# A decoder layer with an mLSTM: another place in memory and another queue for its first head's loads

## Chip, cores and metric

The kernel runs on one core of one Trainium2 chip. The metric is the device time of one execution in microseconds (us), as a median of several. Lower is better.

## What is computed

One hybrid decoder layer over 1024 tokens of width 1024, all in f32. It has three parts, each added to the residual `x`, with a shift, a scale and a gate that are made from a vector `c` for each part:

```
x = x + 0.5*(1+gate0) * swiglu_1(norm(x))
u = norm(x) @ w_in                              # inputs of both kinds of heads
x = x + (1+gate1) * concat(attention(u), mlstm(u)) @ w_out
x = x + 0.5*(1+gate2) * swiglu_2(norm(x))
```

The middle part has 4 heads of differential attention and 4 heads of an mLSTM, each 128 wide. The mLSTM's queries and keys come from `u` through a causal convolution over 4 tokens and a silu; its values come from `u` directly. The mLSTM is computed in chunks:

```
W   = (q k^T) * exp(D - m)                      # in a chunk, masked
num = e_inter * (q C) + W v                     # C: state of 128x128 carried on
h   = num / max(|den|, exp(-m))
C   = decay * C + k^T (w * v)
out = sigmoid(o) * rmsnorm(h) * g
```

where `o`, the output gate, is another product of `u`.

## The kernel before

The kernel is written on a framework that takes instructions in program order, gives tiles their addresses, sets the semaphores, and plans the order of the instructions of each engine: it plays the program on its own clock, and an engine takes the earliest instruction, in program order, of those that are ready by that clock. `high_priority` moves instructions up. An engine then runs its list strictly in order. DMAs are listed on the queue of the engine that issues them: SP (`nc.sync`), ScalarE (`nc.scalar`) or GpSimd (`nc.gpsimd`).

Matrix products are made of three passes each, with a high and a low part of both operands (`mm3`, lines 192 to 194), and two by two blocks are multiplied by Winograd's scheme (`wino`). In the order of the program, the middle of the kernel does this:

- products for values, queries and keys of attention, which are stored to DRAM (`davd`, `qkd`);
- the products of the mLSTM's values, transposed in tiles `vt` and stored to DRAM (`mlv`);
- the products of the mLSTM's queries and keys with the convolution (`conv_handlers`): inputs in tiles `cu`, results in tiles `cv`, stored to DRAM (`mlqk`);
- the products of the output gate (`o_handlers`): each of 8 half heads goes through a tile `vc` (lines 222, 770, 771) and is stored to DRAM (`mlo`, line 772);
- then the pools of all this are closed and new ones opened. `attn_load(0)` loads attention's first head in fourteen DMAs on GpSimd's queue (lines 785 to 789: `oq`, two kinds of `ok`, and `dav`, by halves of 512 tokens), and the heads follow.

`ml_head(h)` is one mLSTM head. It loads keys, queries and values (`mk`, `mq`, `mv`, lines 876 to 878; 512 KB each), head 0 on ScalarE's queue and the others on SP's. `weights` makes decay masks (L889, L891) and their exponentials `mE` (L894), the products of keys and queries (L898), `mW` (L900), and the transposed and weighted keys `kw` (L905, L908). `state` multiplies `kw` with the values (L914), and `read` gathers the outputs in `mn`. In the tail of a head `so` loads the output gate back (L971). `attn_head` does blocks of 128 queries: scores `s` (L807 to L809), maximum, exponentials, transposes and the product with values. The heads of both kinds are independent, so the planner mixes them.

Memory is a stack with two sides. A pool has a range of bytes in every partition, and its tags get rising addresses inside it in the order in which they are first requested; a tag has `bufs` buffers in a row. Pools that come later lie on the bytes of closed ones. With `reuse_waits="tile"`, a tile waits for the users of the earlier tiles on its own bytes. The ranges that matter here, in bytes of a partition, in the kernel before:

| Pool | Tag and range |
|---|---|
| tmp (closed at the boundary) | k: up to 173952 |
| mle (closed at the boundary) | six `vc` of 2048 bytes: 173952 to 186240; two `vt`: 186240 to 190336 |
| nothing at that time | 190336 to 198112 |
| cvp (closed at the boundary) | four `cu`: 198112 to 214604; two `cv`: 214624 to 222816 |
| mlp (opened at the boundary) | mE 170464, mW 174560, mn 178656, mq 186976, mk 195168, mv 203360, mssq 211680, kw 211744, mC 215840, other small ones, so 218720 to 222816 |

In mlp each tag has two buffers (mC four), 4096 bytes each for mq and mk, 4160 for mn and mv, 2048 for mE, mW, kw and so. Head 0 has the first buffer of each and head 1 the second. The gate half that is made last (head 3) is written to the `vc` at 182144; an earlier half of the same head to the one at 173952.

The mE and mW tiles that are requested right after mlp is opened are never written. They only make mE and mW the first tags of the pool.

Of the kernel before, what the change touches and what calls it, by code (L numbers as in the profile page):

```python
# [16 lines left out]
F32 = mybir.dt.float32  # L17
# [8 lines left out]
P = 128  # L26
# [100 lines left out]
class Layer:  # L127
# [739 lines left out]
        return self.y_put(0, h, hf, y)  # L867


    def ml_head(self, h):  # L870
        nc = self.nc
        tl = lambda n, s, **k: self.mlp.tile(s, F32, tag=n, name=n, **k)
        N = tl("mn", [P, 8, 130])
        q, k, v = tl("mq", [P, T]), tl("mk", [P, T]), tl("mv", [P, 8, 130])
        queue = nc.sync if h else nc.scalar
        queue.dma_start(out=k, in_=self.mlqk[4 + h])
        queue.dma_start(out=q, in_=self.mlqk[h])
        queue.dma_start(out=v[:, :, 0:P], in_=self.mlv[h])
        nc.vector.memset(v[:, :, P:130], 1.0)
        sc = P ** -0.5  # L880
        ssq = tl("mssq", [P, 8])
        Ws, kws, Cs = [], [], [None]
# [43 lines left out]
        def read(cs):  # L926
            three = lambda t: t[:, 0:130 * len(cs)].rearrange("p (a b) -> p a b", b=130)
            n = N[:, cs[0]:cs[-1] + 1, :]
            has = [c for c in cs if c > 0]
            I = self.ps()  # L930
            for i, c in enumerate(cs):
                if c > 0:
                    nc.tensor.matmul(I[:, 130 * i:130 * i + 130], cut(q, c), Cs[c], start=True, stop=True,
                                     skip_group_check=True)
            o = cs[0] == 0
            nc.vector.tensor_tensor(out=N[:, has[0]:has[-1] + 1, :], in0=three(I)[:, has[0] - cs[0]:, :],
                                    in1=self.cols[:, 2, has[0]:has[-1] + 1, h:h + 1].broadcast_to([P, len(has), 130]),
# [5 lines left out]
            if o:  # L943
                nc.scalar.copy(out=N[:, 0, :], in_=J[:, 0:130])
            nc.vector.tensor_tensor(out=N[:, has[0]:has[-1] + 1, :], in0=N[:, has[0]:has[-1] + 1, :],
                                    in1=three(J)[:, has[0] - cs[0]:, :], op=ALU.add)
            for c in cs:
                junk = tl("junk2", [P, P], bufs=1)
                nc.scalar.activation(out=junk, in_=N[:, c, 0:P], func=AF.Square, accum_out=ssq[:, c:c + 1])

# [9 lines left out]
        def tail():  # L960
            d, dr, dt = tl("md", [P, 8]), tl("mr", [P, 8]), tl("mt", [P, 8])
            den = N[:, :, P:P + 1].rearrange("p c o -> p (c o)")
            nc.vector.scalar_tensor_tensor(out=d, in0=den, scalar=-1.0, in1=den, op0=ALU.mult, op1=ALU.max)
# [26 lines left out]
def build(tc, yT, **A):  # L990
    nc = tc.nc
    with ExitStack() as es:
        L = Layer(tc, A, es)
# [272 lines left out]
        L.ep = apool("ep", bufs=5)  # L1266
        L.atp = apool("atp", bufs=2)
        L.mlp = rpool("mlp", bufs=2)
        for n in ("mE", "mW"):
            L.mlp.tile([P, 4, P], F32, tag=n, name=n)  # L1270
        L.aops = L.attn_load(0)
        L.ml_tail = lambda: None
        for kind, h in [("m", h) for h in range(4)] + [("a", h) for h in range(4)]:
# [105 lines left out]
```

## Time and profile before

| What | us |
|---|---|
| median of 3 runs (2024.95 to 2032.16) | 2028.65 |
| the profiled execution | 2029.4 |
| its span in the trace | 2027.6 |

The mean granted clock of TensorE was 0.978 of full speed in the profiled execution. Times in the views are microseconds from the start of the span, `x` is a count of instructions, and L898 is line 898 of the kernel. PE is TensorE, PEld its weight loads, DVE VectorE, ACT ScalarE, POOL GpSimd and SP the sync engine; a `q` behind a name means its queue of DMA issues. PEclk is the clock that TensorE was granted, as a part of full speed. The landing of a DMA is recorded for GpSimd's queue alone; for the others it shows in what waits for it.

### The profile page before, as it was taken

The numbers are of one execution on the slowest core, as the hardware profiler recorded it, in microseconds if no ns is written. First come the engines' busy times: TensorE is split into PE (matmuls) and PEld (weight loads), VectorE is DVE, ScalarE is ACT, GpSimd is POOL, SyncE is SP. The second block draws the span as 40 slices with busy tenths as digits, with TensorE's granted clock in tenths as the row PEclk, the third lists the DMA queues.
The fourth block names the chain that finished last, engine by engine and source line by source line (L and its number), as shares of the span: only waits on it lengthen the run. The fifth ranks groups of instructions, "written<-read, shape, count | busy, mean of one in ns | idle before, by whom it ended". The sixth has DMA issues, their size and how long they took to land.

```text
span 2027.6 us, 24626 instructions
## 1 busy us (share of the span) xinstructions
PE 1930.5 (95%) x8898; PEld 1591.1 (78%) x8898; DVE 1463.2 (72%) x2609; ACT 771.0 (38%) x1492; POOL 289.2 (14%) x249
## 2 busy tenths in 40 slices
PE   4999999999999989989997988989999999999999
PEld 3778888888888877877786877876888888888887
DVE  8998888677766689568874885479766655655665
ACT  4522232222232366334444875355222232222232
POOL 0111212211121100000002111003212111121120
PEclk9999999999999999989998999999999999999999
DMA  8344333223221242323439763121111111111113
GB/s 303 122 148 135 120 118 106 84 83 104 99 73 58 94 148 94 99 88 130 146 103 218 158 114 115 54 82 63 63 63 42 63 63 42 50 55 53 53 63 124
DMA packets 86633, 202.35 MB, mean 100 GB/s; under 512 B 10016, under 2 KB 18656, under 8 KB 86512
## 3 DMA queue, kind: packets, MB, share of 16 engines
q1 hardware_dynamic: 77344, 184.46, 27.0%
q0 software_dynamic: 7840, 14.75, 4.2%
q8 instruction: 70, 1.15, 0.2%
q10 hardware_dynamic: 1328, 1.57, 0.2%
q14 instruction: 51, 0.42, 0.1%
HBM read 173.52 MB, written 27.30 MB: 99 GB/s over the span
## 4 chain that ended last, share of the span: by engine, by line
PE 82%; DVE 9%; DMA 4%; ACT 3%; issue 1%; POOL 1%; SPq 0%; DVEq 0%; ACTq 0%; POOLq 0%
PE mm L192 25%; PE mm L193 25%; PE mm L194 25%; DMA qkd<-qhi 1%; PE t L834 1%; DVE adaacc L317 1%; DVE S L371 1%; DMA adac<-in_wada 1%; DVE wlo L181 1%; PE s L807 1%; ACT S L373 1%; PE mm L889 1%; DMA mv<-mlv 1%; DVE nm L811 1%; POOL sf L187 1%
## 5 line engine op out<-in xcount | busy, mean ns | idle before, releaser
L180 ACT CAST whi<-wraw 128x512 fp32r<-128x512 f32 x308 | 190.8, 621 | 479.2 <-PE mm L193 447.1
L192 PE MATMUL mm<-S,whi 128*128 128x512 f32 x900 | 353.3, 393 | 1.3 <-ACT whi L180 0.9
L193 PE MATMUL mm<-S,whi 128*128 128x512 f32 x900 | 352.2, 392 | 0.0
L194 PE MATMUL mm<-S,wlo 128*128 128x512 f32 x900 | 351.4, 391 | 0.3 <-DVE wlo L181 0.3
L522 DVE SCALAR_TENSOR_TENSOR x<-mm,gate,x 128x512 f32<-128x512 f32 x368 | 269.5, 745 | 93.5 <-PE mm L194 92.2
L180 ACT CAST whi<-sf 128x512 fp32r<-128x512 f32 x224 | 138.8, 621 | 397.5 <-PE mm L193 380.4
L181 DVE TENSOR_TENSOR wlo<-wraw,whi 128x512 fp32r<-128x512 f32 x300 | 210.5, 703 | 87.8 <-ACT whi L180 75.9
L193 PE MATMUL mm<-glo,whi 128*128 128x512 f32 x672 | 262.1, 390 | 0.0
L194 PE MATMUL mm<-ghi,wlo 128*128 128x512 f32 x672 | 260.7, 390 | 0.0
L192 PE MATMUL mm<-ghi,whi 128*128 128x512 f32 x672 | 260.5, 392 | 0.1
L187 POOL TENSOR_TENSOR sf<-wraw 128x512 f32<-128x512 f32 x84 | 119.7, 1426 | 602.5 <-DMA wraw<-in_w 413.9
L192 PEld LDWEIGHTS mm<-S,whi 128*128 128x128 f32 x900 | 170.1, 189 | 37.6 <-ACT whi L180 1.7
L194 PEld LDWEIGHTS mm<-S,wlo 128*128 128x128 f32 x900 | 170.0, 189 | 37.1 <-DVE wlo L181 1.8
L193 PEld LDWEIGHTS mm<-S,whi 128*128 128x128 f32 x900 | 170.1, 189 | 35.3 <-DVE S L422 0.2
L181 DVE TENSOR_TENSOR wlo<-sf,whi 128x512 fp32r<-128x512 f32 x224 | 157.8, 704 | 36.9 <-ACT whi L180 36.2
L194 PEld LDWEIGHTS mm<-ghi,wlo 128*128 128x128 f32 x672 | 126.6, 188 | 26.4
L192 PEld LDWEIGHTS mm<-ghi,whi 128*128 128x128 f32 x672 | 126.5, 188 | 26.5 <-ACT ghi L515 0.6
L193 PEld LDWEIGHTS mm<-glo,whi 128*128 128x128 f32 x672 | 126.7, 189 | 26.1
L222 DVE TENSOR_TENSOR c<-w,mm 128x512 f32<-128x512 f32 x84 | 57.2, 685 | 99.5 <-PE mm L194 99.4
L187 POOL TENSOR_TENSOR sf<-wraw,sf 128x512 f32<-128x512 f32 x42 | 62.2, 1482 | 442.9 <-DVE wlo L181 354.9
L317 DVE SCALAR_TENSOR_TENSOR adaacc<-adac,cs,adaacc 128x256 f32<-128x256 f32 x196 | 109.5, 559 | 12.5 <-DMA adac<-in_wada 11.3
L192 PE MATMUL mm<-B11h,whi 128*128 128x512 f32 x248 | 99.9, 410 | 9.0 <-ACT B11h L376 7.2
(341 smaller groups left out, 3413.8 us busy)
## 6 DMA issues: line engine op xcount, KB each, us to landing
wraw<-in_w SPq DMA_DIRECT2D x142, 512.0 KB
adac<-in_wada SPq DMA_DIRECT2D x112, 256.0 KB
ok<-qkd POOLq DMA_DIRECT2D x32, 256.0 KB, 9.4
adaraw<-in_wada SPq DMA_DIRECT2D x12, 512.0 KB
wraw<-in_wo SPq DMA_DIRECT2D x12, 512.0 KB
x<-in_xT SPq DMA_DIRECT2D x16, 256.0 KB
xd<-x SPq DMA_DIRECT2D x16, 256.0 KB
wraw<-in_wqk SPq DMA_DIRECT2D x8, 512.0 KB
```

Source lines behind the costliest of these rows:

```text
L180: nc.scalar.copy(out=hi, in_=raw)
L181: (eng or nc.vector).tensor_tensor(out=lo, in0=raw, in1=hi.bitcast(F32), op=ALU.subtract)
L187: self.sums.tensor_tensor(out=s, in0=a, in1=b, op=op)
L192: nc.tensor.matmul(ps, whi, xhi, start=first, stop=False, skip_group_check=True)
L193: nc.tensor.matmul(ps, whi, xlo, start=False, stop=False, skip_group_check=True)
L194: nc.tensor.matmul(ps, wlo, xhi, start=False, stop=last, skip_group_check=True)
L222: add = lambda o, a, b: nc.vector.tensor_tensor(out=o, in0=a, in1=b, op=ALU.add)
L317: nc.vector.scalar_tensor_tensor(out=acc, in0=raws[k], scalar=self.cs[:, k:k + 1], in1=acc, op0=ALU.mult, op1=ALU.add)
L371: eng.tensor_tensor(out=h, in0=x, in1=r, op=ALU.mult)
L373: self.nc.scalar.activation(out=h, in_=h, func=AF.Identity, scale=self.G[:, g:g + 1], bias=self.mod[:, s:s + 1])
L522: self.nc.vector.scalar_tensor_tensor(out=x, in0=ps, scalar=self.gate[:, g:g + 1], in1=x, op0=ALU.mult, op1=ALU.add)
L807: nc.tensor.matmul(s[:, c0:c1], lhs, k1[:, c, c0:c1], start=True, stop=False, skip_group_check=True)
```

## The change

Head 0's loads move from `ml_head` into a method of their own, `ml_load`, which is called right after mlp is opened and ahead of `attn_load(0)`, and they are issued on GpSimd's queue. The other heads call the same method where their loads were, with SP's queue. The two requests that made mE and mW the first tags of mlp are gone; `ml_load` requests mq, mk and mv, in this order, before any other tag of mlp. The DMAs themselves, their order (keys, queries, values) and their sizes stay, as does all arithmetic.

```diff
--- before.py
+++ after.py
@@ -867,16 +867,21 @@
         return self.y_put(0, h, hf, y)
 
 
-    def ml_head(self, h):
+    def ml_load(self, h, queue):
         nc = self.nc
         tl = lambda n, s, **k: self.mlp.tile(s, F32, tag=n, name=n, **k)
-        N = tl("mn", [P, 8, 130])
         q, k, v = tl("mq", [P, T]), tl("mk", [P, T]), tl("mv", [P, 8, 130])
-        queue = nc.sync if h else nc.scalar
         queue.dma_start(out=k, in_=self.mlqk[4 + h])
         queue.dma_start(out=q, in_=self.mlqk[h])
         queue.dma_start(out=v[:, :, 0:P], in_=self.mlv[h])
         nc.vector.memset(v[:, :, P:130], 1.0)
+        return q, k, v
+
+    def ml_head(self, h):
+        nc = self.nc
+        tl = lambda n, s, **k: self.mlp.tile(s, F32, tag=n, name=n, **k)
+        q, k, v = self.mlops if h == 0 else self.ml_load(h, nc.sync)
+        N = tl("mn", [P, 8, 130])
         sc = P ** -0.5
         ssq = tl("mssq", [P, 8])
         Ws, kws, Cs = [], [], [None]
@@ -1266,8 +1271,7 @@
         L.ep = apool("ep", bufs=5)
         L.atp = apool("atp", bufs=2)
         L.mlp = rpool("mlp", bufs=2)
-        for n in ("mE", "mW"):
-            L.mlp.tile([P, 4, P], F32, tag=n, name=n)
+        L.mlops = L.ml_load(0, nc.gpsimd)
         L.aops = L.attn_load(0)
         L.ml_tail = lambda: None
         for kind, h in [("m", h) for h in range(4)] + [("a", h) for h in range(4)]:
```

## Rows read from the trace of the kernel before

**Rows 1.** the page, busy time, share of the span, instructions of each engine

```profile
PE 1930.5 (95%) x8898; PEld 1591.1 (78%) x8898; DVE 1463.2 (72%) x2609; ACT 771.0 (38%) x1492; POOL 289.2 (14%) x249
```

**Rows 2.** busy time by stretch: us, engines, PEclk, DMA share, GB/s

```profile
1070.00:1080.00 10.00, 3.15 (x17) 1.96 (x15) 1.22 (x4) 3.05 (x6) 0.12 (x1) 0.78 1.25 310
1080.00:1090.00 10.00, 5.66 (x28) 4.99 (x28) 3.00 (x9) 1.84 (x8) 0.00 (x0) 0.67 0.90 289
1090.00:1100.00 10.00, 10.00 (x56) 8.55 (x56) 4.43 (x12) 5.88 (x24) 0.54 (x2) 0.69 0.16 55
1100.00:1200.00 100.00, 97.18 (x716) 83.57 (x714) 87.78 (x262) 79.15 (x272) 23.82 (x41) 1.00 0.74 137
1200.00:1290.00 90.00, 79.82 (x461) 66.27 (x462) 54.26 (x143) 47.28 (x128) 12.82 (x12) 0.98 0.44 107
```

**Rows 3.** waits of TensorE from 1045 to 1104: total, times, longest

```profile
PE mm L898 <- DMA mq<-mlqk: 8.8, 1, 8.8
PE mm L914 <- DMA mv<-mlv: 2.4, 1, 2.4
```

**Rows 4.** timeline of the boundary: start, us, engine, line, operation [idle before]

```profile
1056.65 0.61 POOL L785 DMA_DIRECT2D oq<-qkd  x1 [49.08 <-PE mm L194]
...
1069.29 0.83 POOL L789 DMA_DIRECT2D dav<-davd  x1 [0.88 <-DMA ok<-qkd]
...
1071.38 0.63 ACT L770 ACTIVATE vc<-vc 128x512 f32<-128x512 f32 x1 [2.08 <-DVE vc L222]
1071.39 0.35 ACTq L876 DMA_DIRECT2D mk<-mlqk  x1
...
1072.56 0.32 SPq L772 DMA_DIRECT2D mlo<-vc  x1
...
1072.73 0.42 PE L807 MATMUL s<-ok,oq 128*128 128x128 f32 x2
1072.97 0.38 SPq L971 DMA_DIRECT2D so<-mlo  x1
1073.45 0.38 SPq L876 DMA_DIRECT2D mk<-mlqk  x1
...
1075.73 0.59 ACTq L878 DMA_DIRECT2D mv<-mlv  x1
...
1080.79 0.56 SPq L971 DMA_DIRECT2D so<-mlo  x1
1081.91 2.04 PE L898 MATMUL mm<-mq,mk 128*128 128x128 f32 x8 [8.76 <-DMA mq<-mlqk]
...
1084.45 0.46 PE L808 MATMUL s<-ok,oq 128*128 128x128 f32 x1
...
1084.84 1.14 ACT L908 ACTIVATE kw<-mm,cols 128x128 f32<-128x128 f32 x4 [6.05 <-PE mm L905]
...
1087.83 0.91 PE L914 MATMUL mm<-mv,kw 128*128 128x130 f32 x6 [2.44 <-DMA mv<-mlv]
```

**Rows 5.** the chain that ended last, two pieces: start, us, what

```profile
1067.22 8.48 DMA mlo<-vc
1075.73 11.96 DMA mv<-mlv
```

**Rows 6.** busy time in stretches of 2 us, columns as in rows 2

```profile
1076.00:1078.00 2.00, 0.00 (x0) 0.00 (x0) 0.00 (x0) 1.63 (x3) 0.00 (x0) 0.50 1.09 386
1082.00:1084.00 2.00, 2.00 (x10) 2.00 (x11) 0.00 (x0) 0.00 (x0) 0.00 (x0) 0.50 1.02 380
1088.00:1090.00 2.00, 2.00 (x12) 1.46 (x11) 0.99 (x3) 0.00 (x0) 0.00 (x0) 0.83 0.09 33
```

**Rows 7.** line 785, a load of attention's on GpSimd's queue: issue, landing

```profile
L785 POOL DMA_DIRECT2D oq<-qkd x16: 590/614/674, 1056.6 to 1199.7; - x16
DMA to landing us min/median/max: 3.8/8.2/15.1
```

**Rows 8.** waits of SP's queue from 1045 to 1104, one of them

```profile
SPq L971 <- DMA mlo<-vc: 1.7, 1, 1.7
```

## The prediction

> **What bounds the kernel now.** I read the page first: TensorE is busy 95% of the span [rows 1], so time is lost only where its queue stands still. The table by stage then shows where, near this change: TensorE is busy 3.15 of the 10 us from 1070 and 5.66 of the next 10 us, so 11.2 us stand idle there, and it is back at 97% from 1100 [rows 2]. Before 1070 it works on the output gate's products, after it on the first mLSTM head and the first attention head. The wait view names what it waited for: 8.8 us for the load of the queries and 2.4 us for the load of the values, together the 11.2 us [rows 3]. The granted clock was 0.78, 0.67 and 0.69 in the three 10 us stretches from 1070 and 0.50 in the idle middle, so the work behind the wait also ran at the lower level for a while [rows 2, 6].
>
> The timeline shows how the loads come to be late [rows 4]. ScalarE's queue issues the keys at 1071.39, right behind its last gate activation, and the values at 1075.73. The products that need queries and keys (L898) start at 1081.91, kw is ready four activations from 1084.84 (0.29 us each, so 1085.98), and the state products (L914) start at 1087.83, when the values have landed. The chain of waits has the same two links: a gate store of 8.48 us, then the value load of 11.96 us [rows 5]. Both are long because the DMA engines are full: attention's fourteen loads go out from 1056.65 to 1069.29 on GpSimd's queue [rows 4], and the bytes flow without a pause until 1088, where the rate falls to 33 GB/s [rows 6].
>
> **The change, part by part.** *Addresses.* In the table of bytes above, a pool's tags take rising addresses in the order of their first request. The old placeholders made mE and mW the first tags, so keys and values of head 0 came to lie at 195168 and 203360, on the convolution's tiles or the gap below them. Without the placeholders the first three tags are mq, mk, mv, from the pool's lowest byte. I work out: mq at 170464 and 174560, mk at 178656 and 182752, mv at 186848 and 191008. That is not the convolution's range (198112 up) but the output gate's `vc` tiles (173952 to 186240). So by the sizes the edit does the reverse of its words. Head 0's keys (178656 to 182752) reach into the `vc` tile at 182144, which holds the last gate half, the one that is stored last, at 1072.56. Head 0's queries reach into the one at 173952, and its values lie on old `vt` tiles that have long been stored. mE, mW and mn move onto free ground; as their writers are not late today (mE is done four activations after 1077, its reader waits for L898) that is worth nothing.
>
> *The queue.* Three issues leave ScalarE and go to GpSimd. ScalarE's part is nothing: it waits for TensorE or DMA all through 1072 to 1084. In program order they stand ahead of attention's loads, but each engine's order is planned by readiness: attention's loads have all been issued by 1069.29 while the same plan puts the keys behind the last gate activation (1071.38), and SP issues `so` at 1072.97 ahead of the next head's keys at 1073.45 although the code asks for those first [rows 4]. So I take GpSimd's order to be fourteen attention loads, then keys, queries, values.
>
> *The new wait.* The keys wait for the last gate store, and the queries and values stand behind them on GpSimd, where nothing else is due (the next use is at the third attention block). The next head's keys and queries on SP wait for gate stores too. When does that store land? At the earliest 1072.56 + 3.8, the shortest landing of a 256 KB load on that queue [rows 7] = 1076.4. At the latest 1080.8: today SP issues the second `so` at 1080.79 after a wait for this store [rows 4, 8]. With ScalarE's two loads out of its way but attention's last ones still there I take 1078.
>
> From there to the queries: the fixed part of a load is 3.8 less 256 KB at 390 GB/s (0.7) = 3.1 us [rows 6, 7]. Keys and queries are 1.05 MB. At 390 GB/s for them alone that is 2.7 us, at half of it, beside the next head's loads on SP, 5.4 us. Queries land at 1076.4 + 3.1 + 2.7 = 1082.2 at best, 1080.8 + 3.1 + 5.4 = 1089.3 at worst, and 1078 + 8.5 = 1086.5 as I take it (half rate, since both queues are then released by the same store). Values follow 1.3 to 2.7 us later. The state products need kw, which today comes 4.1 us after the queries (1081.91 to 1085.98), so they start at 1086.3, 1093.4 or 1090.6, against 1087.83: -1.5, +5.6, and +2.8 us as taken. So the wait on the values vanishes, and a later wait on queries takes its place.
>
> *Issue cost.* Three issues on GpSimd cost 0.61 us each [rows 7] and lie inside the 3.1 us. GpSimd's issue took 0.59 to 0.67 us in 16 cases, beside a VectorE that was 88% busy from 1100 to 1200 [rows 2, 7]. The Trainium skill, SBUF — State Buffer, section "SBUF: two separate sides", speaks against the move: a load issued from GpSimd can be held while VectorE runs in a mode that locks a shared port, about 620 ns becoming about 3100. By that page the three issues would cost an estimated 7.4 us more. The trace doesn't show such a hold, and VectorE is idle in the stretch in question, as the wait at L898 is what it waits for.
>
> *Sum.* The profiled execution took 2029.4 us (span 2027.6 and 1.8 around it), 0.75 above the median of 2028.65. Behind the boundary TensorE's order is fixed and 97% busy to 1200, 89% to 1290 [rows 2], so a later start of the first head moves the end nearly one to one. Removed: 0. Added: +2.8. That is 2032.2 against the profile and 2031.5 against the median.
>
> **The rivals.**
> *A. GpSimd's queue does run in program order (slower).* Then attention's loads stand behind keys that wait for a store, from 1056.65 to about 1076.4. Keys and queries come at their best (1082.2), but attention's first seven loads (1.8 MB) share some 4.9 MB with six others from 1078 on, 12.6 us at 390 GB/s and 3.1 fixed: they are there at about 1093, against 1084.45, when the first block's second product ran [rows 4]. TensorE has the mLSTM head alone meanwhile. Price: up to 9 us, 3 if that head fills most of the gap; I take +6, 2034.7. It decides as soon as one key load stands ahead of an attention load on the queue. Against it speaks the planned order seen above.
> *B. The planner lets attention's blocks run ahead (faster).* TensorE's queue has the first block's L807 at 1072.73 and then L898, so L808 stands behind a load for 11.7 us [rows 4]. If the plan, which now has the loads on the same queue behind attention's, expects them late, it places several attention blocks first. Their data are there by about 1078, and up to 8 us of the idle time fills with work that is needed anyway; the mLSTM starts later, which costs little. Price -1 to -8, taken -5: 2023.7. For it: the order is free there. Against it: in the plan of before the second half of the block was put behind the loads.
> *C. The words are true*: the three tiles lie on early ground and are loaded before 1070. Then 8.8 + 2.4 us go [rows 3], 2017.5, or up to 3 us less with the clock up. Against it stand the addresses.
> *D. The issues are held on GpSimd.* By rows at most 3 x 0.08 us (0.67 less 0.59) [rows 7], no change; the page named above would make it 2038.9.
> *E. The plan changes elsewhere* behind the boundary, by more than 6 us either way.
>
> **How the numbers follow.** Forecast 0.50 (its own range 2027 to 2034.3, and 3 us more on both sides for a different interleaving later), A 0.13, B 0.23, C 0.05, D 0.02, E 0.07. Predicted 2031.5. The range of 8 in 10 reaches from B's far end, -8 (2021), to A's far end and the forecast's upper end with its 3 us (2039); outside lie C, most of E and slivers of A and B, about 0.14. Within 0.3% (6.1 us, about what a measurement of this kernel can tell from no change) means 2022.6 to 2034.7. Faster: C 0.05, a third of B 0.07, half of E 0.04 = 0.16. Slower: half of A 0.07, a fifth of the forecast 0.10, half of E 0.04 = 0.21. The rest, 0.63, is no change.
>
> **What would show it.** In the profile after: the three load issues on GpSimd behind attention's last, the first of them at 1076 to 1081 and waiting for `mlo<-vc` (right), ahead of attention's first (A), or before 1070 (C). TensorE's wait at L898 ends at 1082 to 1089, and the wait for the values at L914 is gone. If the idle time from 1070 to 1090 falls clearly under 11 us while the loads still come late, it is B, and `s` products of later blocks stand ahead of L898. A wrong layout, that is key tiles with no wait for a gate store, would overturn all of it.

## The result, and the profile after

The changed kernel took 2014.14 us (median of 4 runs, 2010.34 to 2015.20) beside 2028.78 us (2024.95 to 2032.16) for the kernel before: a ratio of 0.9921, 95% interval 0.9902 to 0.9939. By the ratio it is 16.0 us faster (12.4 to 19.9), and it lies below the forecast range. Its profiled execution took 2013.82 us with a span of 2012.0. Line numbers behind the edit are five higher: L898 is L903, L914 is L919, L889 is L894, the loads L876 to L878 are L874 to L876.

The page gives TensorE nearly the busy time it had [rows 1], in a span 15.6 us shorter:

```profile
PE 1924.0 (96%) x8898; PEld 1586.9 (79%) x8898; DVE 1468.5 (73%) x2609; ACT 769.7 (38%) x1492; POOL 294.2 (15%) x252
```

The timeline of the boundary in the kernel after (start, us, engine, line, operation, idle before it) answers to [rows 4]:

```profile
1064.25 0.79 POOL L789 DMA_DIRECT2D dav<-davd  x1 [0.88 <-DMA ok<-qkd]
...
1065.75 0.48 PE L894 MATMUL mm<-negm,ident 32*128 32x128 f32 x2
...
1067.23 1.28 ACT L899 ACT_TABLE_LOAD   x1
1068.52 1.14 ACT L899 ACTIVATE mE<-mm,cols 128x128 f32<-128x128 f32 x4
1069.54 0.38 ACT L813 ACTIVATE e<-s,nm 128x128 f32<-128x128 f32 x1
...
1070.07 0.47 PE L807 MATMUL s<-ok,oq 128*128 128x256 f32 x1 [1.35 <-ACT e L813]
...
1073.12 0.74 PE L834 MATMUL t<-dav,at 128*128 128x128 f32 x2
...
1074.92 0.55 POOL L874 DMA_DIRECT2D mk<-mlqk  x1 [9.89 <-DVE e L823]
1075.46 0.54 POOL L875 DMA_DIRECT2D mq<-mlqk  x1
1076.23 0.91 POOL L876 DMA_DIRECT2D mv<-mlv  x1 [0.23 <-issue]
...
1078.63 0.50 PE L830 MATMUL t<-ident,e 128*128 128x128 f32 x3
1082.93 1.18 PE L903 MATMUL mm<-mq,mk 128*128 128x128 f32 x8 [3.80 <-DMA mq<-mlqk]
...
1088.14 0.89 PE L919 MATMUL mm<-mv,kw 128*128 128x130 f32 x6
```

GpSimd's order is the one that was forecast: fourteen attention loads, then keys, queries, values, the keys after a wait of 9.89 us. But TensorE's queue is another one. Where only the first products (L807) of attention's first block stood ahead of L898, the scores of four and a half blocks now stand ahead of L903, with the transposes and products of the first of them. So the loads come late, as forecast, and little waits for them (TensorE's waits from 1045 to 1104, which answer to [rows 3]: total, times, longest):

```profile
PE mm L903 <- DMA mq<-mlqk: 3.8, 1, 3.8
PE s L807 <- ACT e L813: 1.8, 2, 1.4
```

To compare kernels I count from the first product at the boundary (L889 before, L894 after; "the start" below), as single executions reach it at different times, with the same program up to there: 1070.6 before, 1065.8 after, 1067.6 to 1073.2 in the kernels below that put nothing new ahead of it. Stretches of the kernel before, columns as in [rows 2]: the first 30 us, the next 100, the time from the last mLSTM product to attention's last output, and all from the start to the end:

```profile
1070.60:1100.60 30.00, 18.81 (x102) 15.59 (x102) 9.26 (x27) 11.33 (x39) 1.14 (x3) 0.72 0.74 214
1100.60:1200.60 100.00, 96.58 (x712) 83.24 (x711) 87.78 (x261) 78.60 (x272) 23.55 (x40) 1.00 0.75 138
1199.60:1290.70 91.10, 80.77 (x469) 66.95 (x468) 55.11 (x144) 47.29 (x129) 13.08 (x12) 0.98 0.45 109
1070.60:2027.60 957.00, 918.67 (x4441) 760.58 (x4440) 622.52 (x1130) 374.11 (x833) 166.60 (x141) 0.98 0.28 80
```

The same four of the kernel after:

```profile
1065.80:1095.80 30.00, 24.33 (x136) 19.49 (x136) 16.43 (x39) 17.95 (x55) 10.49 (x17) 0.83 1.20 264
1095.80:1195.80 100.00, 96.88 (x699) 83.48 (x697) 84.07 (x249) 76.78 (x263) 18.55 (x31) 0.97 0.74 132
1204.30:1277.00 72.70, 68.59 (x386) 57.01 (x385) 46.47 (x114) 35.38 (x96) 10.83 (x8) 0.98 0.30 105
1065.80:2012.00 946.20, 916.31 (x4441) 758.77 (x4440) 625.33 (x1130) 373.44 (x833) 170.69 (x144) 0.99 0.28 81
```

From the start to the end it is 10.8 us shorter (957.0 less 946.2) with the same 4441 products: TensorE's idle time fell from 38.3 to 29.9 us and its busy time by 2.4. The idle time went in two places. In the first 30 us it fell from 11.2 to 5.7. Behind the last mLSTM product it fell from 10.3 (91.10 less 80.77) to 4.1. There attention has little left beside it: in both kernels 157 products of the mLSTM's outputs with `w_out` ("output projection" below). But 386 products stand there in all, in place of 469, and the 83 that are missing are attention's. Of the 11.7 us of these two places 3.3 came back in others, most of it behind attention's last output (14.1 to 16.6).

The granted clock was higher in the first 30 us (0.83 for 0.72), but the fall in busy time doesn't come from there. Up to attention's last output the same products kept TensorE busy for longer, at the same mean clock (the kernel before, then the kernel after); what fell lies behind it, 722.8 to 718.4 us:

```profile
1070.60:1290.70 220.10, 195.91 (x1278) 165.73 (x1278) 151.15 (x428) 137.22 (x439) 37.18 (x53) 0.95 0.62 136
1065.80:1277.00 211.20, 197.91 (x1278) 167.15 (x1278) 155.47 (x428) 136.74 (x438) 39.87 (x56) 0.95 0.64 141
```

What TensorE waits for in the last stretch of the four, behind the last mLSTM product, before and then after:

```profile
PE s L807 <- ACT e L813: 5.3, 8, 1.7
PE t L834 <- ACT at L831: 2.2, 3, 1.1
PE t L864 <- DVE O L861: 1.9, 2, 1.5
```

```profile
PE t L864 <- DVE O L861: 1.6, 1, 1.6
PE t L834 <- ACT at L831: 0.8, 1, 0.8
PE s L807 <- ACT e L813: 0.8, 2, 0.4
```

These are the exponentials, copies and norms of attention itself: with no mLSTM products left to put between, TensorE waits for ScalarE and VectorE. The other 4.8 us between the two spans lie ahead of the start, in a part that the edit doesn't touch. Most of them are busy time of the same products (1011.8 to 1007.7 us), which runs from 1006.4 to 1014.3 us in the kernels below. The medians' 14.6 us is more than the 10.8, and one pair of profiles can't place the rest.

### The profile page after: what moved, and what is told of

Read it like the earlier page. It is cut to its first block, busy times and chain, and to the rows that moved or that the text cites. A ratio compares the mean times of both kernels' runs of the same rounds, so it can differ in the third digit from the quotient of the medians.

```text
span 2012.0 us, 24629 instructions
## 1 busy us (share of the span) xinstructions
PE 1924.0 (96%) x8898; PEld 1586.9 (79%) x8898; DVE 1468.5 (73%) x2609; ACT 769.7 (38%) x1492; POOL 294.2 (15%) x252
## 4 chain that ended last, share of the span: by engine, by line
PE 84%; DVE 8%; DMA 3%; ACT 3%; issue 1%; POOL 1%; SPq 0%; DVEq 0%; ACTq 0%; POOLq 0%
PE mm L192 26%; PE mm L193 26%; PE mm L194 26%; PE t L834 1%; DVE adaacc L317 1%; DVE S L371 1%; DMA adac<-in_wada 1%; DVE wlo L181 1%; ACT S L373 1%; PE s L807 1%; POOL sf L187 1%; PE t L830 1%; PE s L808 1%; PE mm L894 1%; DMA qkd<-qhi 1%
## 5 line engine op out<-in xcount | busy, mean ns | idle before, releaser
L317 DVE SCALAR_TENSOR_TENSOR adaacc<-adac,cs,adaacc 128x256 f32<-128x256 f32 x196 | 109.7, 560 | 14.4 <-DMA adac<-in_wada 13.2
```

The lines of the kernel that those rows point to most:

```text
L317: nc.vector.scalar_tensor_tensor(out=acc, in0=raws[k], scalar=self.cs[:, k:k + 1], in1=acc, op0=ALU.mult, op1=ALU.add)
```

## The experiments

Three theories stood at first. O: TensorE's order at the boundary pays. P: the new places of the tiles pay. Q: the queue, or the traffic on it, pays. Idle times below are TensorE's, in the first 30 us from the start, the next 100, and the rest to the end.

| kernel | what differs | ratio to before, 95% interval | start to end, us | idle, us |
|---|---|---|---|---|
| before | | 1 | 957.0 | 11.2 / 3.4 / 23.7 |
| after | | 0.9921 (0.9902 to 0.9939) | 946.2 | 5.7 / 3.1 / 21.1 |
| e1_places | before, places of after | 1.0009 (0.9997 to 1.0020) | 958.3 | 13.9 / 2.7 / 25.0 |
| e2_queue | after, places of before | 0.9901 (0.9887 to 0.9916) | 939.5 | 1.9 / 3.6 / 20.0 |
| e5_undo | after, old order | 0.9994 (0.9978 to 1.0009) | 955.8 | 14.4 / 3.0 / 24.0 |
| e6_ahead | before, four blocks ahead | 0.9941 (0.9927 to 0.9956) | 946.6 | 7.3 / 2.3 / 24.9 |
| e9_ahead2 | before, two blocks ahead | 0.9928 (0.9902 to 0.9955) | 946.3 | 6.5 / 4.5 / 20.8 |
| e7_own | loads on the convolution's tiles | 0.9962 (0.9948 to 0.9976) | 954.2 | 5.6 / 7.6 / 20.4 |
| e7b_own_sp | the same, SP's queue | 0.9968 (0.9949 to 0.9988) | 952.8 | 6.2 / 7.0 / 22.6 |
| e8_own_ahead | e7b and four blocks ahead | 0.9913 (0.9890 to 0.9935) | 943.1 | 2.8 / 4.7 / 22.1 |
| e10_cover | before, last mLSTM head held back | 0.9993 (0.9979 to 1.0007) | 957.7 | 10.8 / 2.3 / 24.8 |
| e11_six | e2, six blocks ahead | 0.9926 (0.9906 to 0.9947) | 945.9 | 2.8 / 4.3 / 21.1 |
| e12_vgap | before, VectorE work in the gap | 1.0011 (0.9996 to 1.0025) | 960.1 | 11.3 / 3.4 / 23.8 |
| e13_vmid | before, VectorE work behind it | 1.0020 (1.0004 to 1.0036) | 962.3 | 11.3 / 6.2 / 26.0 |
| e14_clear | e7b, mE, mW, first kw off the gate's tiles | 0.9957 (0.9944 to 0.9971) | 951.5 | 1.1 / 7.9 / 22.2 |
| e15_clear_ahead | e14 and four blocks ahead | 0.9921 (0.9899 to 0.9943) | 944.9 | 2.1 / 4.2 / 21.5 |

### One part alone

e1_places takes the two placeholders away and asks for the load tiles first, with the loads in the head and on ScalarE's queue as before:

```diff
-        for n in ("mE", "mW"):
-            L.mlp.tile([P, 4, P], F32, tag=n, name=n)
...
-        N = tl("mn", [P, 8, 130])
         q, k, v = tl("mq", [P, T]), tl("mk", [P, T]), tl("mv", [P, 8, 130])
+        N = tl("mn", [P, 8, 130])
```

> The places alone: the placeholders are gone and mq, mk, mv are the first tags of the pool, so they lie as in the changed kernel, but head 0's loads stay on ScalarE's queue. TensorE's queue has the order of before (L807, then the products of keys and queries, then L808). Theory O (the gain is the order on TensorE's queue: attention's first blocks ahead of the first mLSTM products): no gain, and the loads wait for the last gate stores, so 2029 to 2035 us, +0 to +6 over before. Rival P (the places pay): about 2014. Rival Q (the queue and its traffic pay): about 2029, as before.

e2_queue is the changed kernel with placeholders that keep every tile where it lay before:

```diff
+        for n, s in (("mE", [P, 4, P]), ("mW", [P, 4, P]), ("mn", [P, 8, 130])):
+            L.mlp.tile(s, F32, tag=n, name=n)
         L.mlops = L.ml_load(0, nc.gpsimd)
```

> The queue alone: head 0's loads go by GpSimd's queue as in the changed kernel, but placeholders for mE, mW and mn keep every tile of the pool at its place of before. TensorE's queue has the order of the changed kernel. Theory O: the whole gain and a little more, because the keys lie on ground that is free early and their load goes out right behind attention's last (at about 1065 instead of 1075): the 3.8 us that are left of the wait for the queries shrink to 0 to 1, so 2008 to 2014 us. Rival P: about 2029, as before. Rival Q: about 2014.

The places alone, 1.0009, are no gain; the queue, 0.9901, is all of it. (In e2_queue the loads are also called ahead of attention's in the program, as in the changed kernel. No run moves the queue without the call, so "the queue" means both here.) TensorE's order is the old one in e1_places and the new one in e2_queue. In e1_places the tiles on the gate's ground make the loads late and TensorE waits for them (its wait from 1045 to 1104, then the issues on ScalarE's queue, with a start at 1071.1):

```profile
PE mm L898 <- DMA mq<-mlqk: 13.6, 1, 13.6
```

```profile
1079.24 0.35 ACTq L876 DMA_DIRECT2D mk<-mlqk  x1
1079.63 0.44 ACTq L877 DMA_DIRECT2D mq<-mlqk  x1
1080.11 0.59 ACTq L878 DMA_DIRECT2D mv<-mlv  x1
```

In e2_queue the keys go out 0.3 us after the start and no wait for a DMA is left in the first 30 us. P falls; O and Q go together here, so the order had to be moved by itself.

### The order alone

e5_undo is the changed kernel with the second product (L808) of attention's first block held behind the key transposes of the first mLSTM head, without a semaphore, so that TensorE's queue has the order of before:

```diff
+                    if h == 0 and i == 0:
+                        self.tc.add_manual_dep(m.ins, self.kmark.ins.name, mybir.DependencyInfo(
+                            mybir.DependencyClass.NoSync, mybir.DependencyReason.DATA), reason="order")
```

> The changed kernel with one thing undone: the first attention block's second product (L808) has to stand behind the transposes of head 0's keys on TensorE's queue. The rest of TensorE's queue then comes out in the order of before; places, queue and waits of the loads are those of the changed kernel. Theory O: the gain is gone, and the later loads cost what the prediction said, 2029 to 2036 us. Rivals P and Q: the gain stays, about 2014 to 2016.

e6_ahead is the kernel before, its places and ScalarE's queue kept, with attention's first four blocks traced first and L898 held behind their last transposes. e9_ahead2 does it with two blocks:

```diff
+        first = L.attn_blocks(0)
+        for _ in range(4):
+            next(first)
+        L.amark0 = L.amark.ins.name
...
+                if c == 0 and h == 0:
+                    self.tc.add_manual_dep(m.ins, self.amark0, ...)
```

> The kernel before with the order alone: four blocks of attention's first head are traced ahead of the mLSTM, and the first product of keys and queries has to stand behind their last transposes on TensorE's queue. Places and queue of the loads are those of before. Theory O: most of the gain without the change, 2011 to 2018 us. Rivals P and Q: no gain, 2026 to 2031.

> The kernel before with two attention blocks ahead of L898 in place of four (places and queue of before). Theory O: two blocks hold about half the work of four (with four, -11 us), so the gap is filled for some 4 to 6 us: 2022 to 2026, a gain of 0.15 to 0.35%. If the first block or two are what counts because they cover all of the wait for the queries (8.8 us): 2016 to 2020, as with four. If the gain comes only with order further on: 2026 to 2031.

With the old order the change is worth nothing (0.9994), though queue and places are the changed kernel's; with the new order the kernel before gains 0.6 to 0.7% without either. O holds, P and Q fall. e5_undo also shows the forecast's own case: the keys wait for the last gate store, and L898 (L906 there) for the queries (GpSimd's issue in the timeline, then TensorE's wait):

```profile
1078.94 0.55 POOL L877 DMA_DIRECT2D mk<-mlqk  x1 [9.66 <-DMA mlo<-vc]
```

```profile
PE mm L906 <- DMA mq<-mlqk: 14.4, 1, 14.4
```

Two blocks can't be told from four: 0.9928 and 0.9941, with intervals that overlap, and the expectation that two would give half falls. In e6_ahead TensorE waits for the first exponentials where after it hardly does (TensorE's wait from 1065 to 1104, then ScalarE's rows, start at 1071.3):

```profile
PE s L807 <- ACT e L813: 6.0, 2, 5.7
```

```profile
1076.49 0.59 ACTq L883 DMA_DIRECT2D mv<-mlv  x1
1077.11 1.28 ACT L899 ACT_TABLE_LOAD   x1 [4.36 <-DMA mlo<-vc]
1078.41 1.14 ACT L899 ACTIVATE mE<-mm,cols 128x128 f32<-128x128 f32 x4
1079.42 0.39 ACT L813 ACTIVATE e<-s,nm 128x128 f32<-128x128 f32 x1
```

The load of the values stands on ScalarE's queue in front of its exponentials and waits, by the profile for a gate store, so attention's first exponential comes 8.1 us after the start; in the kernel after, with no load on that queue, it comes 3.7 us after it (1069.54 less 1065.8). This is the wait in the trace that goes with the rest of the gain, from 0.9941 here to 0.9901 in e2_queue; no run takes it out of e6_ahead by itself.

### Early loads

e7_own puts rival C of the prediction into effect, tiles on early ground and early loads: the load tiles get a pool of their own, which lies exactly on the convolution's bytes. e7b_own_sp loads them by SP, e8_own_ahead also forces the four blocks ahead:

```diff
-        tl = lambda n, s, **k: self.mlp.tile(s, F32, tag=n, name=n, **k)
+        tl = lambda n, s, **k: self.mlkp.tile(s, F32, tag=n, name=n, **k)
...
+        L.mlkp = rpool("mlkp", bufs=2)
         L.mlp = rpool("mlp", bufs=2)
```

> What the change's words say, made true: the kernel after, but head 0's keys, queries and values (and their successors) come from a pool of their own that lies exactly where the convolution's tiles were, loaded by GpSimd's queue. Their issues should then come well before 1060, wait for no gate store, and L898's products follow the first L889 products without a DMA wait, in the order of before (two heads' parts of the mLSTM ahead of attention's blocks). Theory O (the gap at the boundary costs what TensorE has nothing to do in): the gap is closed by data that are there instead of by other blocks; 9 to 11 us less than before, plus the clock's part, so 2013 to 2020, faster than before by 0.4 to 0.8%. Rival Q' (early loads push attention's own loads and the gate weights' back on the full DMA engines): the idle time comes back at attention's products, 2024 to 2031, no change. Rival R (the order as such pays later on, not at the boundary: attention's blocks and the mLSTM's interleave better behind it): order of before, so no gain, 2024 to 2031, with the stretch from 1200 to 1270 as badly filled as before.

> As the run before (own pool on the convolution's tiles), with head 0's three loads on SP's queue. Theory O: the same time as with GpSimd's queue, within 3 us. Rival D of the prediction (issues on GpSimd are held by VectorE): the run on SP is faster by some 2 us for each held issue, up to 7 us. Rival Q': no change against before, either queue.

> The run before with the four attention blocks put ahead of L898 by force: early loads and the new order together. Theory O (one gap, filled once): the two gains are not added; the same as the better of the two alone, 2010 to 2016. Rival R (order pays by itself later on, early loads pay at the boundary): the gains add, 2000 to 2008. If forced order costs something because blocks then wait for their own exponentials: 2016 to 2022.

The keys are issued at 1045.10 in e7_own, L903 starts 2.2 us after the start, and no wait for a load is left; yet the gain is 0.4 and 0.3%. TensorE's order is the old one in both: in e7_own the first scores come at 1083.63, behind L903 at 1070.64. With the four blocks forced ahead as well (e8_own_ahead) the gain is 0.9%, in O's range; R's sum of two gains, 2000 to 2008 us, was not reached. GpSimd's queue and SP's can't be told apart, so nothing holds an issue on GpSimd for long. But VectorE stood still in e7_own and e7b_own_sp, and the state products (L919) came only when it was done, since the weights mW now lie over a gate tile (VectorE's wait in e7_own from 1045 to 1104):

```profile
DVE mW L905 <- DMA mlo<-vc: 7.3, 1, 7.3
```

So e14_clear orders the pool's tiles so that mE, mW and the first kw lie off the gate's tiles, and e15_clear_ahead forces the four blocks ahead in it:

```diff
-            kw = tl("kw", [P, 4, P])
+            kw = tl(f"kw{hf}", [P, 4, P], bufs=1)
...
+        for n, sh, k in (("mn", [P, 8, 130], 2), ("mssq", [P, 8], 2), ("so", [P, HT], 2), ("mC", [P, 130], 4), ("junk2", [P, P], 1), ("kw1", [P, 4, P], 1)):
+            L.mlp.tile(sh, F32, tag=n, name=n, bufs=k)
```

> The own pool for the loads on SP's queue, and mE, mW and the first kw moved off the gate tiles too, so that nothing of the first mLSTM head waits for a gate store; order of TensorE as without the blocks ahead (mLSTM first). Theory O (idle time at the boundary is what pays, whatever fills it): idle time in the first 30 us down to 1 to 3 us, 2010 to 2016, as fast as the changed kernel. Rival V (attention's blocks must run early, since VectorE and ScalarE pace them to the end): idle time at the boundary goes as above, but the last mLSTM product stands behind the 44th half block, some 10 us stay idle behind it, and the gain is half or less: 2018 to 2025.

> As e14_clear with four attention blocks forced ahead of the first mLSTM products. Theory O: the same as e14_clear within 3 us. Rival V: 6 us or more faster than e14_clear, 2008 to 2014, as e8_own_ahead or better by up to 4 us.

Stretches of e14_clear, divided as above:

```profile
1069.60:1099.60 30.00, 28.90 (x175) 23.68 (x175) 18.50 (x54) 19.32 (x72) 9.39 (x16) 0.83 0.85 190
1099.60:1199.60 100.00, 92.08 (x660) 79.69 (x659) 85.77 (x254) 76.16 (x253) 19.72 (x33) 0.97 0.80 139
1188.80:1284.30 95.50, 85.39 (x479) 70.60 (x478) 61.31 (x153) 48.49 (x132) 13.22 (x13) 0.95 0.43 107
1069.60:2021.10 951.50, 920.28 (x4441) 762.65 (x4440) 619.66 (x1128) 374.80 (x833) 171.49 (x145) 0.98 0.28 78
```

The gap is closed: 1.1 us idle in place of 11.2, less than in the kernel after. Still the gain is 0.43%, about half of what the same kernel has with attention ahead (0.79%; the intervals don't meet). Both runs lie in V's ranges (2021.8 and 2012.8 us), and O in its bare form, that any filling will do, falls. Part of the idle time came back. The next 100 us lose 7.9 us in place of 3.4, and behind the last mLSTM product 479 products are left, 157 of them the output projection's, with 10.1 us idle. TensorE's waits in those 100 us:

```profile
PE t L864 <- DVE O L861: 4.2, 3, 1.9
PE s L807 <- ACT e L813: 2.0, 2, 1.4
```

The reading that fits these waits: a gap filled with mLSTM products uses up what would later stand between attention's dependent steps, and a gap filled with attention's own blocks takes them away from the place where TensorE waits for ScalarE and VectorE. One thing stays unclean: in e14_clear VectorE stood 5.1 us on a gate store once more (mC lies over it), before attention's first maximum was due.

### Is the end worth anything by itself?

e10_cover leaves the boundary of before alone and holds the last mLSTM head back among attention's blocks. In TensorE's queue the last mLSTM product stands behind the 46th of 64 score tiles before, the 53rd after, and the 54th here:

```diff
+        L.marks, L.holds = {}, {('QK', 0): (2, 1), ('QC', 3): (2, 4), ('QC', 6): (2, 6)}
...
+                self.hold(m, h, ("QK", c))
```

> The kernel before with everything at the boundary as it was (places, ScalarE's queue, order of TensorE up to the last mLSTM head), but the last mLSTM head's products held back among attention's: its last product comes behind the 54th of attention's 64 half blocks, as in the changed kernel, in place of behind the 46th. Theory O+E (the change's gain has two parts, the gap at the boundary filled with attention's products, and fewer attention blocks left alone at the end, where TensorE waits for exponentials): the second part alone, idle time behind the last mLSTM product falls from 10 us to some 4 to 6 us, so 2022 to 2026, a gain of 0.2 to 0.35%, with the 11 us at the boundary still there. Theory O (the gap alone): no change, 2027 to 2032. Rival V (VectorE and ScalarE are what the whole stretch waits for, so what is taken away at the end is waited for in the middle): no change in the time, but the idle time moves from the end into the stretch before it.

The first 30 us, the stretch behind the last mLSTM product, and start to end of e10_cover:

```profile
1073.20:1103.20 30.00, 19.16 (x99) 15.91 (x98) 8.66 (x26) 10.83 (x39) 0.53 (x2) 0.66 0.73 212
1219.70:1293.30 73.60, 67.09 (x372) 56.33 (x371) 40.93 (x107) 33.19 (x87) 10.13 (x8) 0.96 0.30 103
1073.20:2030.90 957.70, 919.78 (x4441) 763.82 (x4440) 616.30 (x1130) 374.43 (x833) 167.89 (x141) 0.98 0.28 80
```

There are 372 products behind the last mLSTM product, fewer still than after, and no gain: 0.9993, at most 0.2% by its interval. Attention's last output comes 220.1 us after the start, as before. Idle time behind the last mLSTM product did fall, from 10.3 to 6.5 us. But up to that output it is only 2.5 us less in all, and the same products kept TensorE busy 2.4 us longer (198.3 us for 195.9), with the granted clock at 0.66 in place of 0.72 in the first 30 us. So the second saving didn't show as one of its own. That attention's blocks have to be done earlier, and that the gap is the time for it, is what e14_clear and e15_clear_ahead point to; this run doesn't show it.

e11_six puts six blocks ahead in e2_queue:

```diff
+        L.marks, L.holds = {}, {('QK', 0): (0, 5)}
```

> The fastest kernel so far (queue of the change, places of before), with six attention blocks ahead of the first mLSTM head's products in place of four and a half; the last mLSTM product comes behind the 55th half block in place of the 53rd. Theory O+E: the gap was already filled (1.9 us idle in its 30 us), two half blocks fewer stand alone at the end, and the boundary now has attention alone, waiting for its exponentials: 2008 to 2014, the same as with four and a half. Rival V (the earlier VectorE gets its work the better, without end): 2002 to 2008. If too much attention alone at the boundary costs what it saves at the end and more: 2014 to 2020.

0.9926: not better than four and a half, rather worse than e2_queue's 0.9901, though the intervals overlap. What is longer in its profile lies behind attention's last output, 742.1 us against 736.0: 24 products of the output projection that in e2_queue stand among attention's come only there. How many blocks are best is not settled by these runs.

### VectorE's share

e12_vgap and e13_vmid add to the kernel before ten VectorE operations on a tile that nothing reads, in the gap or one each in ten attention blocks behind it:

```diff
+                nc.vector.scalar_tensor_tensor(out=self.vj, in0=self.vj, scalar=f[:, 0:1], in1=self.vj, op0=ALU.mult, op1=ALU.add)
```

> The kernel before with ten added VectorE operations of 128x512 (0.69 us each by the profile, 6.9 us in all, results unused) that become ready at the boundary, while TensorE waits for the loads. Theory V (behind the boundary VectorE and ScalarE are as short as TensorE, and the gap is time of theirs that is lost too): VectorE is idle there, so no change, 2027 to 2032. If the added work holds up the first weights or attention's first maximum: 2 to 4 us longer.

> The kernel before with the same ten operations, one in each of ten attention blocks of the second and third head, in the stretch where TensorE is 97% and VectorE 88% busy. Theory V: most of the 6.9 us reach the end: 2033 to 2038, slower by 0.15 to 0.4%. Rival O (TensorE alone bounds that stretch; VectorE's free 12% take the work): no change, 2027 to 2032.

The ten of e13_vmid by its trace (duration ns min/median/max, first and last start):

```profile
L822 DVE SCALAR_TENSOR_TENSOR vj<-vj,f x10: 732/744/753, 1131.0 to 1190.1; 128x512 f32<-128x512 f32 x10
```

7.4 us of VectorE cost 4.1 us (0.8 to 7.3) behind the gap, and 2.2 (-0.8 to 5.1) in it. The first is a cost, though TensorE is 97% and VectorE only 88% busy there; the second can't be told from none. The two intervals overlap, so that VectorE's time is dearer behind the gap is likely and not shown.

## Why the prediction was wrong, step by step

*Right: addresses and GpSimd's order.* The keys wait for the last gate store (9.66 us in e5_undo, where the profile names it; in the kernel after it names a VectorE operation), behind attention's fourteen loads. The tiles don't lie on early ground, as worked out.

*Right: how late the loads are.* Counted from the start, L898 was forecast at 15.9 us (1086.5 less 1070.6) and came at 17.1 in the kernel after, 17.0 in e5_undo and 16.3 in e1_places. The state products were forecast at 20.0 and came at 20.4 and 19.8 in the last two. The first of the three issues came at 9.1 in the kernel after, taken at 7.4 and within its 5.4 to 10.4. The three took 2.0 us, against 1.8.

*Not borne out: the later start passes to the end "nearly one to one".* The two kernels in which just that happens, e1_places and e5_undo, are 1.8 us longer (-0.6 to 4.1) and 1.2 us shorter (-4.5 to 1.8). The 2.8 us lie inside the first interval and outside the second. TensorE's idle time from the start to the end did rise, by 3.3 and 3.1 us, so it wasn't filled further on; but the same products kept it busy 2.0 and 4.3 us less in these two profiles, and no run shows why.

*Wrong, and what decided: TensorE's order was taken as given.* The sum says "TensorE's order is fixed" and "Removed: 0": it was made with the order of before, and rival B got 0.23. What the runs show in its place is four and a half blocks ahead of L903 and a gain of 0.8%, which is gone (0.9994) when the old order is forced back. The argument against B, that the plan of before put the block's second half behind the loads, spoke of a plan with the loads on ScalarE's queue. e1_places (ScalarE's queue, old order) and e2_queue (GpSimd's, new order) show that the queue, with the earlier call, moves the order and the places don't. In e7_own, with the same queue and call but loads that are early, the order is the old one again. That the plan counts the loads behind attention's fourteen on the same queue, and so expects them late, was B's reason; the runs agree with it and don't show the planner's numbers. The sign set for B came true: less idle time at the boundary while the loads are still late.

*Wrong: B's size.* It was taken at -5 us, at most -8; measured are some -16 (-12.4 to -19.9). It counted only the idle time of the boundary, 5.5 us of which went. It left out that the blocks moved there are missing behind the last mLSTM product (10.3 us idle to 4.1). With what came back elsewhere the two profiles show 8.4 us less idle time; the rest of the 16 is not placed.

*Wrong: "ScalarE's part is nothing".* ScalarE's idle time was read as no demand. It was held: the load of the values stood ahead of its exponentials on its queue for 4.3 us (row below, of the kernel before). With the old order that is worth nothing (0.9994 in e5_undo), as forecast; once attention's blocks are first, TensorE waits for them (5.7 us in e6_ahead).

```profile
1076.36 1.28 ACT L894 ACT_TABLE_LOAD   x1 [4.34 <-DMA mlo<-vc]
```

*Rival C, likely too large.* Early loads were priced at all the waits, -11.2 us. Put into effect, they gave -7.7 (-4.9 to -10.5), -6.5 (-2.4 to -10.3) and, with the gap closed to 1.1 us, -8.7 (-5.9 to -11.4), so the last interval just holds the price. What is shown is that the filling counts: e15_clear_ahead, with 2.1 us idle in the gap, is faster than e14_clear with 1.1 (0.9921 against 0.9957).

*Rival D, small as its rows said.* e7_own and e7b_own_sp differ by 0.06%. Four GpSimd issues at 1077.26 to 1079.03 in the kernel after did take 1.04 to 1.07 us, next to a busy VectorE, against 0.59 to 0.67 in [rows 7], but they start 0.58 to 0.60 us apart, so the queue kept its pace. The Trainium skill, SBUF — State Buffer, section "SBUF: two separate sides", has about 3100 ns for a DMA issued from GpSimd beside a VectorE copy that holds the shared port. No run here shows an issue that long, and the traces don't say whether a VectorE operation here holds that port.

## What to carry to other kernels

Where a planner writes each engine's order, moving a load to another queue and to an earlier place in the program can reorder an engine that the edit never names: price that first, and settle it by forcing the old order into the new kernel. Idle time on the bounding engine is best filled with the work that would otherwise stand at the end with too little beside it. A load on a compute engine's queue that has to wait holds that engine's own work, and its idle time in the trace then looks like lack of demand.

## What the runs showed of the hardware

In e2_queue, where 1.9 us stand idle in the first 30, the granted clock was 0.89 there; before, with 11.2 us idle, it was 0.72, and 0.50, the lower of the two levels (1.2 of 2.4 GHz), in the idle middle [rows 6]. How much stood idle doesn't give the clock by itself: e14_clear, with 1.1 us idle, had 0.83. The work behind the idle time ran slower with it: the eight products of keys and queries took 2.04 us before, at 0.50 [rows 4, 6], and 1.06 us in e2_queue, at 1.00 (its first 30 us, the stretch of these products, and their row):

```profile
1068.60:1098.60 30.00, 28.09 (x176) 22.88 (x176) 21.66 (x53) 23.07 (x71) 10.93 (x18) 0.89 1.30 284
1081.84:1083.00 1.16, 1.16 (x13) 1.16 (x12) 1.05 (x4) 1.09 (x4) 1.16 (x3) 1.00 1.01 353
1081.84 1.06 PE L903 MATMUL mm<-mq,mk 128*128 128x128 f32 x8
```

What this was worth to the whole is not shown. TensorE's busy time from the start to the end was 918.7 us before and 914.0 in e2_queue, but also 914.4 in e5_undo, which has 14.4 us idle in its first 30.

And the same program reaches the boundary at times that differ by 7.4 us (1065.8 to 1073.2) in the single executions shown here, on several chips, nearly half of what the edit gains: stretches of two profiles are compared from a common event, not by the clock of the span.
